# Weights of a later product split during the attention and kept in DRAM, and two column blocks of that product begun without one row block

## The chip, the core and the metric

The kernel runs on one core of one Trainium2 chip. The core has engines that each follow their own queue of instructions and meet through semaphores: TensorE (PE in the profile; its weight loads are PEld), VectorE (DVE), ScalarE (ACT), GpSimd (POOL) and SyncE (SP). Here SP computes nothing: it issues the DMAs of `load` and `store`, in its order. PE's work here is matrix products and the transposes by which tiles are turned. The metric is the device time of one execution in microseconds, as the median of several executions. All data is float32.

## What is computed

Two layers run on 640 tokens: 512 of one prompt and 128 of eight sample streams with 16 each. Layer 0 is stick-breaking attention over keys of the stream (and, for the samples, 512 cached keys each); layer 1 is gated linear attention (GLA). Each layer normalises its input, scales and shifts it by values from a conditioning vector, projects it, mixes, multiplies by a gate, projects back and adds to the residual.

```python
for i in range(DEPTH):                       # two layers
    shift, scale, gate = jnp.split(c @ w_ada[i] + b_ada[i], 3, axis=-1)
    h = rmsnorm(x, norm_g[i]) * (1 + scale[:, None]) + shift[:, None]
    if i % N_MIXERS == 0:                    # layer 0: 16 heads of 128
        y, k, v = sb_mixer(h, sb_w_in[j], sb_w_out[j], cache_sb_k[j], cache_sb_v[j])
    else:                                    # layer 1: 4 heads, keys of 256, values of 512
        y, S = gla_mixer(h, gla_w_in[j], gla_w_a2[j], gla_b_a[j], gla_norm_g[j], gla_w_out[j], S0)
    x = x + gate[:, None] * y

def sb_mixer(...):
    q, k, v, zg = jnp.split(h @ w_in, 4, axis=-1)
    ...
    y = (o * jax.nn.silu(zg.astype(jnp.float32))).astype(h.dtype) @ w_out

def gla_mixer(...):
    q, k, v, r, a_lr = jnp.split(h @ w_in, [nk, 2 * nk, 2 * nk + nv, 2 * nk + 2 * nv], axis=-1)
```

The change touches the time from the attention of layer 0 to the first product of layer 1, which is the first 512 columns of `v` in `gla_mixer`.

## The kernel before, in words

**Products.** A float32 product is made of three products of a faster type (`float32r`): each operand x is split by `halves` into hi (a cast, on ACT, L134) and lo = x - hi (a subtraction, on DVE, L135), and hi*hi + hi*lo + lo*hi is added up in PSUM. Weights come as raw tiles `wr` of 128x1024 (512 KB) by `wraw` and are split by `wsplit` into `wh` and `wl`, two buffers each; during the change of layers `ring3` gives every third piece the tiles `s0`, `s1` instead (the rows then say `s`). The 640 tokens are five row blocks `a` of 128: 0 to 3 are the prompt, 4 the samples.

**Attention.** Two lanes for the prompt (`prompt_lane`, one per head of a pair) and one for the samples (`sample_lane`) go through eight pairs of heads. The sample lane has 32 units: four per pair, two streams in each. A unit loads four blocks of cached keys and values (`kc` twice, `vc` twice), turns the keys on PE (L1100, 2 x 8 transposes), which ACT and DVE copy to `kt` (L1102), makes the scores (L1114, L1119), sends them through ACT and DVE (`stick`: a sigmoid pair on ACT, L963 and L964, a scan on DVE, L967, then L1120 to L1130), turns the weights (L1137, and L1138 for `a_new`, once in a unit), and multiplies by the values (L1152). The next unit's scores stand behind L1138 in PE's order. Beside them runs a filler, so that PE has work while a lane waits: first the products of two gates (`plain`, L650), then `share(g)`, the output projection of the attention in four parts `g` of four heads (two pairs) each. A share has 240 matmuls of 128x512 (L696), four groups of columns `c` by five row blocks by twelve; it needs the two pairs' outputs. Shares 0 to 2 are the filler as far as the lanes last, and run bare behind them. `y_t[a, c]`, the sums of the shares, lie in the slots t0 to t19 (`5 * c + a`).

**Order.** PE's order is written by hand: a `drive` runs the filler and `side.tick` puts lanes' steps between its matmuls by a planned clock `pe["now"]`; `side.until` runs lanes alone until a condition holds. DVE, ACT and POOL have a written order only from `in_order` on (the change of layers); elsewhere, and for SP everywhere, a scheduler places them.

**Change of layers.** `share(3)` ends a column block of the residual in each step (`add`): three DVE operations, a square on ACT for the norm, a DMA of x to DRAM, then `turn` (four transposes, L1327, and copies into `xp`, L1329) and, after the last column block, `norm(a)` (a `rstd_w` on DVE, turned by PE at L244). `last_gate` makes half of layer 1's gate meanwhile from 16 tiles `ar` of 512 KB (L1290). Then comes `six`: the first GLA product with eight blocks `j` of 256 rows of the weights, 30 matmuls each (six for a row block, L515). Its two first `j` are begun before everything is normalised: `most(j)` scales and splits the row blocks 1 to 4, then the product runs for blocks 1, 3, 4, 2 of j=0 and j=1; `rest(j)` adds row block 0, which is normalised last. From j=2 on, `until(j)` makes the scaled operands of the next `j` (`make`: `scale` of j+2, `part_up` of j+1) between the products, and the weights of the next `j` are loaded raw and split. Behind it come the products of a small matrix (`wa`, L1424) and the queries.

## Time and profile before

| what | value |
|---|---|
| median of three executions | 2473.24 us (2471.8 to 2477.05) |
| the profiled execution, its own time | 2472.03 us |
| its span in the profile | 2470.1 us |
| mean granted TensorE clock | 0.995 of full speed |
| PE busy | 2408.5 us, 98% of the span |
| DVE busy | 1581.7 us, 64% of the span |
| share of PE on the chain that ended last | 85% (DVE 4%, ACT 3%, DMA 2%) |

The page counts an engine as busy while it executes; ends of PE's instructions are modelled, so "busy" says where PE had work, and time is better read from starts of instructions far apart. A "pair" below is the stretch from one `a_new` transpose to the fourth after it. In rows of the trace `x24` is a count, a bracket at the end is idle time before the row with what ended it, `PEclk` is the granted clock and `DMA share` the mean busy share of the core's 16 DMA engines.

### The profile page before, as it was taken

How to read it: one execution, taken by the hardware profiler on the slowest of the kernel's cores; microseconds unless marked ns; L12 is line 12 of the kernel's file. 1: busy time of each engine (PE TensorE's matmuls, PEld its weight loads, DVE VectorE, ACT ScalarE, POOL GpSimd, SP SyncE). 2: the span in 40 equal slices, each digit the busy share in tenths (PEclk: the TensorE clock that was granted, in tenths of full speed). 3: DMA queues.
4: the chain of work that ended last, by engine and by line, in shares of the span. 5: the costliest groups of instructions: out<-in, count | busy, mean ns of one | idle time of the engine just before them, and what ended most of it. 6: DMA issues, size and time to landing. Idle time of an engine off the chain costs nothing.

```text
span 2470.1 us, 44598 instructions
## 1 busy us (share of the span) xinstructions
PE 2408.5 (98%) x17817; PEld 2141.9 (87%) x17817; DVE 1581.7 (64%) x2580; ACT 993.3 (40%) x1711; POOL 156.6 (6%) x405
## 2 busy tenths in 40 slices
PE   7999999999999999999999999999999999999998
PEld 4689999999999999888887767999999989977776
DVE  5765655555556656766776578766676566676556
ACT  4432222222223335555544245433333555565223
POOL 0010000000000000000000010000000132332000
PEclk8999999999999999999999999999999999999999
DMA  9966666766664348777774564444434678976634
GB/s 344 370 218 213 210 216 199 239 210 225 210 197 128 109 145 274 259 241 235 254 235 147 187 234 129 136 123 125 134 111 114 175 247 264 303 261 224 220 115 149
DMA packets 477841, 502.12 MB, mean 203 GB/s; under 512 B 26618, under 2 KB 386434, under 8 KB 477506
## 3 DMA queue, kind: packets, MB, share of 16 engines
q1 hardware_dynamic: 449042, 440.80, 56.2%
q0 software_dynamic: 14432, 46.67, 5.5%
q10 hardware_dynamic: 14160, 11.80, 1.4%
q8 instruction: 140, 2.29, 0.4%
q14 instruction: 67, 0.55, 0.1%
HBM read 410.05 MB, written 89.13 MB: 202 GB/s over the span
## 4 chain that ended last, share of the span: by engine, by line
PE 85%; DVE 4%; ACT 3%; DMA 2%; issue 1%; POOL 0%; SPq 0%; ACTq 0%; POOLq 0%; DVEq 0%
PE ps_mm L591 43%; PE ps_mm L696 11%; PE ps_mm L650 10%; PE ps_mm L365 3%; PE ps_tp L1100 2%; PE ps_tp L1579 2%; PE ps_tp L1152 1%; PE ps_tp L1056 1%; PE ps_z L1032 1%; PE ps_z L180 1%; PE ps_mm L2088 1%; PE ps_z L1114 1%; PE ps_z L222 1%; PE ps_tp L677 1%; PE ps_mm L515 1%
## 5 line engine op out<-in xcount | busy, mean ns | idle before, releaser
L591 PE MATMUL ps_mm<-sums,wh 128*128 128x320 f32 x2752 | 613.6, 311 | 1.5 <-ACT wh L134 1.5
L591 PEld LDWEIGHTS ps_mm<-sums,wh 128*128 128x128 f32 x2752 | 458.0, 188 | 10.4 <-issue 7.4
L591 PE MATMUL ps_mm<-h,wh 128*128 128x320 f32 x2064 | 461.4, 311 | 0.8 <-DVE u L597 0.8
L591 PE MATMUL ps_mm<-sums,wl 128*128 128x320 f32 x1376 | 425.2, 309 | 0.7 <-DVE wl L135 0.7
L135 DVE TENSOR_TENSOR wl<-wr,wh 128x1024 fp32r<-128x1024 f32 x193 | 236.2, 1225 | 211.1 <-ACT wh L134 208.1
L591 PEld LDWEIGHTS ps_mm<-h,wh 128*128 128x128 f32 x2064 | 343.2, 188 | 15.7 <-issue 11.0
L134 ACT CAST wh<-wb 128x1024 fp32r<-128x1024 f32 x170 | 178.4, 1049 | 431.8 <-PE ps_mm L591 368.2
L134 ACT CAST wh<-wr 128x1024 fp32r<-128x1024 f32 x193 | 202.5, 1050 | 324.8 <-PE ps_mm L591 186.8
L591 PE MATMUL ps_mm<-h,wl 128*128 128x320 f32 x1032 | 318.9, 309 | 0.0
L650 PE MATMUL ps_mm<-h,wh 128*128 128x320 f32 x1152 | 263.5, 316 | 3.5 <-DVE out L597 2.4
L591 PEld LDWEIGHTS ps_mm<-sums,wl 128*128 128x128 f32 x1376 | 258.3, 188 | 1.0 <-DVE wl L135 1.0
L135 DVE TENSOR_TENSOR wl<-wb,wh 128x1024 fp32r<-128x1024 f32 x170 | 207.8, 1222 | 51.0 <-ACT wh L134 50.6
L650 PEld LDWEIGHTS ps_mm<-h,wh 128*128 128x128 f32 x1152 | 192.0, 188 | 17.9 <-issue 8.9
L696 PE MATMUL ps_mm<-wh,ogh 128*128 128x512 f32 x450 | 196.8, 437 | 6.2 <-ACT y L704 3.0
L591 PEld LDWEIGHTS ps_mm<-h,wl 128*128 128x128 f32 x1032 | 193.8, 188 | 0.0
L650 PE MATMUL ps_mm<-h,wl 128*128 128x320 f32 x576 | 177.9, 309 | 0.0
L696 PE MATMUL ps_mm<-wh,ogl 128*128 128x512 f32 x450 | 177.0, 393 | 0.3 <-DVE ogl L135 0.3
L696 PE MATMUL ps_mm<-wl,ogh 128*128 128x512 f32 x450 | 177.0, 393 | 0.2 <-DVE wl L135 0.2
L696 PEld LDWEIGHTS ps_mm<-wh,ogh 128*128 128x128 f32 x450 | 84.9, 189 | 34.4 <-issue 15.1
L650 PEld LDWEIGHTS ps_mm<-h,wl 128*128 128x128 f32 x576 | 108.2, 188 | 0.0
L696 PEld LDWEIGHTS ps_mm<-wh,ogl 128*128 128x128 f32 x450 | 84.5, 188 | 20.2 <-DVE ogl L135 0.7
L515 PE MATMUL ps_mm<-wh,h 128*128 128x512 f32 x252 | 90.7, 415 | 5.6 <-ACT h L134 4.0
(370 smaller groups left out, 3719.6 us busy)
## 6 DMA issues: line engine op xcount, KB each, us to landing
ar<-in_w_ada_dram SPq DMA_DIRECT2D x128, 512.0 KB
wb<-in_sb_w_in_dram SPq DMA_DIRECT2D x82, 512.0 KB
ar<-in_w_ada_dram SPq DMA_DIRECT2D x128, 256.0 KB
kc<-in_cache_sb_k_dram SPq DMA_DIRECT2D x64, 512.0 KB
vc<-in_cache_sb_v_dram SPq DMA_DIRECT2D x64, 512.0 KB
wr<-in_gla_w_in_dram SPq DMA_DIRECT2D x51, 512.0 KB
wb<-in_gla_w_in_dram SPq DMA_DIRECT2D x45, 512.0 KB
wr<-in_sb_w_in_dram SPq DMA_DIRECT2D x44, 512.0 KB
```

The source lines that it names most:

```text
L134: nc.scalar.copy(hi, x)
L135: (e or dve).tensor_tensor(lo, x, hi.bitcast(F32), op=ALU.subtract)
L180: mm(acc[32 * q:32 * q + 32, :w], cT[:, kt + m, :], by(cT[:, kt + m, :], rs[m // each][:, m % each, q, :]), start=kt + m == 0, stop=kt + m ...
L222: mm(acc[32 * j:32 * j + 32, :256], cT[:, kt + m, :], by(cT[:, kt + m, :], r[:, 256 * j:256 * j + 256]), start=kt + m == 0, stop=kt + m == ...
L365: mm(acc[a], l[:, c], by(l[:, c], r[:, k2, :]), start=kt == k0 and first, stop=kt == k0 + nk - 1 and last)
L515: mm(acc[a], l, by(l, r[:, e, :]), start=j == 0 and e == 0 and begun, stop=j == 7 and e == 1 and last)
L591: mm(acc, l[:, k, :], by(l[:, k, :], r), start=start and k == 0 and first, stop=k == 7 and last, skip_group_check=True)
L650: mm(acc[nt], l[:, k, :], by(l[:, k, :], r), start=k0 == 8 and k == 0 and first, stop=k0 == 0 and k == 7 and last)
L677: turn_block(tp[:, c:c + P], block(out[hh][:, t0:t0 + P]), ident)
L696: mm(acc, l, by(l, r[:, e, :]), start=i == 0 and e == 0 and first, stop=i == 1 and e == 1 and last)
L1100: turn_block(tp[:, P * c:P * c + P], block(kc[:, c, P * hh:P * hh + P]), ident)
L1579: mm(out, l[a], by(l[a], r[b]), start=start and n == 0, stop=stop and n == 2, skip_group_check=True)
```

## The change

There are three edits.

1. **`presplit`**, a fourth lane during the attention. It starts when the two gates are done. For each of 16 blocks of 128 rows of the first GLA product's weights it loads a 128x512 tile (256 KB), splits it with `halves`, and stores both halves (256 KB each) to new DRAM tiles `six_d`. Its tiles are the slots t14 to t19, in two sets of three. `share(0)` gets a call `at` that, ahead of its third column group, runs lanes alone until all 16 blocks are split, since that group's and the fourth's sums use the same slots.
2. **`made(j)`** takes the place of load and split in `six`: it loads `wh` and `wl` of a block (two loads of 512 KB instead of one), and ACT and DVE no longer split them.
3. **The order at the change of layers.** `most(j)` leaves out row block 3, which `third(j)` adds; j=0 and j=1 begin with blocks 1, 4 and 2, then come (0, 3) and (1, 3) and block 0. `add` of row block 0 in the last column group is kept back (`late`) until `most(0)` is done; (0, 1) of the product, which stands for j=0 and a=1, is begun as soon as share 3's last (1, 3) is added, and so stands ahead of the last turns. The bias of the last gate is added 6 us later in the plan; x and `h21_d` stores of this stage are issued by POOL instead of ACT; `make(2)` and `make(3)` put `part_up` ahead of the next `scale`.

```diff
+    six_d = [[dp.tile([P, 1024], F32, name=f"six_{j}_{n}") for n in range(2)] for j in range(8)]
...
@@ class Quarters: most
-            scaled(t, i, j, ts, bc, P)
+            scaled(t, i, j, ts, bc, P, 3 * P)
+            samples_scaled(t, i, j, ts, bc)
+            yield
...
-            nc.scalar.dma_start(out=h21_d[i][:, j, :], in_=ts[0][:, hs[1]])
+
+        def third(self, i, j, xT, t, bc):
+
+            ts = self.exact[j]
+            scaled(t, i, j, ts, bc, 3 * P, NP)
+            halves(self.upper[j][:, 0, :NP - HALF], self.upper[j][:, 1, :NP - HALF], ts[0][:, HALF:NP])
+            halves(*[x[:, 3 * P:NP] for x in self.whole[j]], ts[1][:, 3 * P:NP])
+            move(h21_d[i][:, j, :], ts[0][:, hs[1]])
@@ six
-        parts = [(j, a) for j in range(first) for a in (1, 3, 4, 2)] + [(j, 0) for j in range(first)]
+        parts = [(j, a) for j in range(first) for a in (1, 4, 2)] + [(j, a) for a in (3, 0) for j in range(first)]
...
+                if made:
+                    if j < 7:
+                        ws[j + 1] = made(j + 1)
@@ attention
+        def presplit():
+            while not state["free"]:
+                yield step(1.0)
+            src1 = A["gla_w_in"][0].rearrange("(kt p) n -> p kt n", p=P)
+            for kt in range(KT):
+                x, *t = [slot(14 + 3 * (kt % 2) + n, (P, 512), dt, "six") for n, dt in enumerate((F32, F32R, F32R))]
+                load(x, src1[:, kt, 2 * NK:2 * NK + 512])
+                yield step(4.0)
+                halves(*t, x)
+                for d, y in zip(six_d[kt // 2], t):
+                    store(d[:, 512 * (kt % 2):512 * (kt % 2) + 512], y.bitcast(F32))
+                yield step(4.0)
+            state["split"] = True
...
-        for x in (prompt_lane(0), prompt_lane(1), sample_lane()):
+        for x in (prompt_lane(0), prompt_lane(1), sample_lane(), presplit()):
...
-            drive(share(g, og0, w_out0))
+            drive(share(g, og0, w_out0, at=lambda c: side.until(lambda: "split" in state) if c == 2 else None))
@@ last_gate
+            yield step(6.0)
             dve.tensor_tensor(bias, acc[:, :256], bias, op=ALU.add)
@@ most, add
-            while min(done[1:]) < 5:
+            while not (normed[1] and normed[2] and normed[4]):
...
+        def add(a, c, pt):
+            if (a, c) == (0, 3):
+                late.append(pt)
+                return
+            summed(a, c, pt)
+            squared(a, c)
+            if (a, c) == (1, 3):
+                next(gemm)
@@ made
+            ws = [(sp if third else wp).tile([P, 1024], F32R, tag=t, name=t[:2], bufs=1 if third else 2)
+                  for t in (ring3["tags"] if third else ("wh", "wl"))]
+            for t, d in zip(ws, six_d[j]):
+                load(t.bitcast(F32), d)
@@ behind share 3
+        side.until(lambda: busy["most"])
+        summed(0, 3, late[0])
+        squared(0, 3)
+        parts(1)
+        for _ in h2.most(1, 1, xT, xp[1], bc, middles[1]):
+            pass
+        parts(2)
+        side.until(lambda: normed[3])
+        for j in range(2):
+            h2.third(1, j, xT, xp[j], bc)
+        parts(5)
+        side.until(lambda: normed[0])
         for j in range(2):
             h2.rest(1, j, xT, xp[j], bc)
+        parts(2)
...
-            if j < 7:
+            if 3 < j < 7:
                 h2.scale(1, j + 1, xT, bc, pairs_of=lambda n: xp[n])
             if j < 8:
                 h2.part_up(1, j, pm.tile([P, 512], F32R, tag=("vhi", "vlo")[j % 2], name="middle")[:, :256])
+            if 2 <= j < 4:
+                h2.scale(1, j + 1, xT, bc, pairs_of=lambda n: xp[n])
```

In PE's order the first edit moves matmuls of the shares. Rows of one sample unit in the middle of the attention, from its scores on, before the change (L696 are the share's matmuls; L1114 and L1119 are the unit's scores, L1152 its values, L1056 and L1049 the prompt lanes):

```order
L1114 MATMUL ps_z<-kt,q_one 32x256 x8
L1119 MATMUL ps_z<-k,q 32x16 x4
L1152 MATMUL ps_tp<-vc,aT_s 32x128 x16
L1152 MATMUL ps_tp<-v,aT_s 32x128 x4
L696 MATMUL ps_mm<-wh,ogh 128x512
L696 MATMUL ps_mm<-wl,ogh 128x512
L696 MATMUL ps_mm<-wh,ogl 128x512
L1056 MATMUL ps_tp<-aT,v 128x128 x3
L1049 MATMUL ps_tp<-ident,s_12067 128x128 x3
L696 MATMUL ps_mm<-wh,ogh 128x512
L696 MATMUL ps_mm<-wl,ogh 128x512
L696 MATMUL ps_mm<-wh,ogl 128x512
```

and the same unit after the change (L1134, L1139, L1172, L1076, L1069, L1052 and L1120 are the lines that were L1114, L1119, L1152, L1056, L1049, L1032 and L1100; L1120 turns the next unit's keys, L1182 belongs to the last unit's values):

```order
L1134 MATMUL ps_z<-kt,q_one 32x256 x8
L1139 MATMUL ps_z<-k,q 32x16 x4
L1172 MATMUL ps_tp<-vc,aT_s 32x128 x16
L1172 MATMUL ps_tp<-v,aT_s 32x128 x4
L1076 MATMUL ps_tp<-aT,v 128x128 x3
L1069 MATMUL ps_tp<-ident,s_12113 128x128 x3
L1052 MATMUL ps_z<-k,q 128x512
L1120 MATMUL ps_tp<-ident,kc 128x128 x8
L1076 MATMUL ps_tp<-aT,v 128x128 x3
L1052 MATMUL ps_z<-k,q 128x512
L1120 MATMUL ps_tp<-ident,kc 128x128 x8
L1182 MATMUL ps_tp<-ident,osb 128x128
```

Of the 32 units, those that had share matmuls before had 21 or 27 each (9 and 12 in the first and the last of them). Now, after the first six of them (120 matmuls, the first two column groups of share 0), eight units have none and the one behind them has 15, so that 192 matmuls that stood in units before stand behind the last unit. In all, PE has as many matmuls as before.

SP's order in the same part of the attention, before:

```order
L71 DMA wr<-in_sb_w_out_dram 128x2x512
L71 DMA vc<-in_cache_sb_v_dram 128x4x256 x2
L71 DMA kc<-in_cache_sb_k_dram 128x4x256 x2
L71 DMA zg<-zd_135 128x1280
L71 DMA vc<-in_cache_sb_v_dram 128x4x256 x2
L71 DMA wr<-in_sb_w_out_dram 128x2x512
L71 DMA kc<-in_cache_sb_k_dram 128x4x256 x2
L71 DMA q<-qd_120 128x1280
L71 DMA k<-kd_128 128x1280
```

and after, from one load of cached values to the next but one (`six` is a tile of presplit; L71 loads, L74 stores; the two stores of a block stand behind its load and so behind its split):

```order
L71 DMA vc<-in_cache_sb_v_dram 128x4x256 x2
L71 DMA kc<-in_cache_sb_k_dram 128x4x256 x2
L71 DMA six<-in_gla_w_in_dram 128x512
L71 DMA zg<-zd_135 128x1280
L74 DMA six_0_149<-six 128x512
L74 DMA six_1_150<-six 128x512
L71 DMA vc<-in_cache_sb_v_dram 128x4x256 x2
L71 DMA six<-in_gla_w_in_dram 128x512
L71 DMA wr<-in_sb_w_out_dram 128x2x512
L71 DMA kc<-in_cache_sb_k_dram 128x4x256
L74 DMA six_0_151<-six 128x512
L74 DMA six_1_152<-six 128x512
```

The 16 loads and 32 stores of presplit lie like this between the loads of nine units: the first right behind the keys of the eighth unit, the last behind those of the seventeenth.

PE's order at the change of layers, from the last matmul of share 3, before (L244 a norm's turn, L1290 the gate, L1327 a turn of x, L515 the GLA product):

```order
L696 MATMUL ps_mm<-s_15826,ogl 128x512
L244 MATMUL ps_tp<-ident,rstd_w 128x128
L1290 MATMUL ps_z<-ar,c_15307 32x256 x8
L1327 MATMUL ps_tp<-ident,y 128x128 x4
L515 MATMUL ps_mm<-wh,h 128x512
L515 MATMUL ps_mm<-wl,h 128x512
L515 MATMUL ps_mm<-wh,h 128x512 x2
L515 MATMUL ps_mm<-wl,h 128x512
L515 MATMUL ps_mm<-wh,h 128x512 x2
```

and after, from the first matmuls of the product (L535 is that line now, L1356 and L1325 are the turn and the gate, L245 the norm):

```order
L535 MATMUL ps_mm<-wh,h 128x512
L1356 MATMUL ps_tp<-ident,y 128x128 x4
L1325 MATMUL ps_z<-ar,c_15451 32x256 x8
L535 MATMUL ps_mm<-wh,h 128x512
L535 MATMUL ps_mm<-wl,h 128x512
L535 MATMUL ps_mm<-wh,h 128x512 x2
L535 MATMUL ps_mm<-wl,h 128x512
L535 MATMUL ps_mm<-wh,h 128x512
L245 MATMUL ps_tp<-ident,rstd_w 128x128
L535 MATMUL ps_mm<-wh,middles 128x512
L535 MATMUL ps_mm<-wl,middles 128x512
L535 MATMUL ps_mm<-wh,middles 128x512
```

Before, the last two groups of the gate and a turn stood ahead of the first matmul of the product. Now its first row block, (0, 1), comes right behind share 3; a turn and the gate's last group follow, then (0, 4), the norm of block 3, and (0, 2), whose halves are the tiles `middles`.

More of the change, by code (lines that the diff above doesn't have):

```diff
@@ L482, in again, with six @@
                     halves(self.upper[n + e][:, 0], self.upper[n + e][:, 1], r[:, e])
-    def six(h, w, n0, acc, until, asked, first=0):
+    def six(h, w, n0, acc, until, asked, first=0, made=None):
         src = w.rearrange("(kt p) n -> p kt n", p=P)
@@ L1263, in hybrid_step_kernel @@
         dve.tensor_copy(cT1[:, :, :NSEQ], c91.rearrange("p r kt -> p kt r"))
-        busy = {"n": 0, "of": 0, "most": 0}
-        done = [0] * TOK
+        busy = {"of": 0, "most": 0}
+        normed = [False] * TOK
+        late = []
         def last_gate():
@@ L1294, in last_gate @@
                 store(gate_d[1][:, 1024 + 256 * j:1280 + 256 * j], bias[32 * j:32 * j + NSEQ, :])
-        def counted(gen, a):
-            busy["n"] += 1
-            yield from gen
-            busy["n"] -= 1
-            done[a] += 1
-        def most():
-            while min(done[1:]) < 5:
-                yield step(0.3)
-            for j in range(2):
-                h2.most(1, j, xT, xp[j], bc, middles[j])
-                yield step(3.0)
-                busy["most"] += 1
+        def most():
+            while not (normed[1] and normed[2] and normed[4]):
+                yield step(0.2)
+            for _ in h2.most(1, 0, xT, xp[0], bc, middles[0]):
+                yield step(0.8)
+            busy["most"] = 1
         bc = po.tile([P, T], F32, name="rstd_bc1")
@@ L1370, in hybrid_step_kernel, with made @@
         acc = []
-        gemm = six(h2, w_in1, 2 * NK, acc, until, lambda: None, 2)
+        def made(j):
+            n = ring3["n"] = ring3["n"] + 1
+            third = ring3["pool"] is not None and n % 3 == 0
+            ws = [(sp if third else wp).tile([P, 1024], F32R, tag=t, name=t[:2], bufs=1 if third else 2)
+                  for t in (ring3["tags"] if third else ("wh", "wl"))]
+            for t, d in zip(ws, six_d[j]):
+                load(t.bitcast(F32), d)
+            return [t.rearrange("p (a n) -> p a n", a=2) for t in ws]
+        gemm = six(h2, w_in1, 2 * NK, acc, until, lambda: None, 2, made)
         def ahead(c):
@@ L1379, in hybrid_step_kernel, with parts @@
         drive(share(3, og0, w_out0, add, ahead, first))
-        acc += [bank("mm") for _ in range(5)]
-        for n in range(8):
-            side.until(lambda: busy["most"] > n // 4)
-            if n == 0:
+        at = {a: bank("mm") for a in (1, 4, 2, 3, 0)}
+        acc += [at[a] for a in range(TOK)]
+        def parts(n):
+            for _ in range(n):
                 next(gemm)
-            next(gemm)
-            side.tick()
-        side.until(lambda: not busy["n"])
+                side.tick()
+        side.until(lambda: busy["most"])
[10 more added lines that the diff above has]
+        side.until(lambda: normed[0])
         for j in range(2):
             h2.rest(1, j, xT, xp[j], bc)
+        parts(2)
+        side.until(lambda: not side.lanes)
         only_d.close()
@@ L1404, in make @@
         def make(j):
-            if j < 7:
+            if 3 < j < 7:
                 h2.scale(1, j + 1, xT, bc, pairs_of=lambda n: xp[n])
```

52 lines of the change are left out of this document (32 added, 20 removed).

## The prediction

> **What bounds the kernel now.** I read first the page's head and its chain of the work that ended last, to see whether there is one engine whose work is the time.
>
> ```profile
> span 2470.1 us, 44598 instructions
> ...
> PE 2408.5 (98%) x17817; PEld 2141.9 (87%) x17817; DVE 1581.7 (64%) x2580; ACT 993.3 (40%) x1711; POOL 156.6 (6%) x405
> ...
> PE 85%; DVE 4%; ACT 3%; DMA 2%; issue 1%; POOL 0%; SPq 0%; ACTq 0%; POOLq 0%; DVEq 0%
> ```
>
> PE is the bound nearly everywhere: 85% of the chain, and busy for all but 62 us of the span. The number of PE's matmuls is the same before and after. So time can come only out of stretches where PE waits, and is lost wherever the change makes PE wait. I therefore read the two stretches that the change touches: the attention, and the change of layers. First the attention, as busy time of the engines in three stretches that run from one `a_new` transpose to another (four units with filler; one unit with only 18 short matmuls of a gate as filler; one with only nine matmuls of a share).
>
> ```profile
> core 0: us, PE busy (x) PEld busy (x) DVE busy (x) ACT busy (x) POOL busy (x), PEclk, DMA share, GB/s
> 1060.81:1110.93 50.12, 50.12 (x504) 40.93 (x503) 35.01 (x85) 29.83 (x67) 1.45 (x14) 1.00 0.75 241
> 1027.39:1036.80 9.41, 9.41 (x125) 8.69 (x123) 3.82 (x12) 5.13 (x11) 0.66 (x4) 1.00 0.79 271
> 1036.80:1048.36 11.56, 8.72 (x100) 5.93 (x99) 10.86 (x30) 6.72 (x16) 0.20 (x2) 1.00 1.00 336
> ```
>
> With its filler PE never waits: 50.12 of 50.12 us. With nine matmuls as filler (third row) it was busy for 8.72 of 11.56 us, though that unit's DVE also did splits that are not its own. What PE waited for in that unit is in its table of waits:
>
> ```profile
> PE ps_tp L1100 <- DVE kt L1102: 1.2, 1, 1.2
> PE ps_tp L1049 <- DVE s L1035: 0.9, 1, 0.9
> PE ps_mm L696 <- ACT ogh L134: 0.4, 1, 0.4
> PE ps_mm L696 <- DVE ogl L135: 0.3, 1, 0.3
> ```
>
> The first two are a unit's own chain, through DVE. The filler is what hides it.
>
> **Part 1: eight units without filler.** The order of PE takes 192 share matmuls out of the sample units and puts them behind the last one. What a unit costs PE without them:
>
> ```profile
> L696 PE MATMUL ps_mm<-wh,ogh 128*128 128x512 f32 x30 | 14.5, 483 | 0.0
> L135 DVE TENSOR_TENSOR wl<-wr,wh 128x1024 fp32r<-128x1024 f32 x3 | 3.7, 1223 | 0.7 <-ACT wh L134 0.7
> ...
> 1372.05 14.13 PE ps_mm L696 x60
> ```
>
> The first row is one of three alike (hi and lo), so four units hold 90 share matmuls, 22.5 a unit. The last row, of the chain, has 60 of them bare in 14.13 us: 0.2355 us each. A filled unit takes 50.12 / 4 = 12.53 us, so PE's own work in it is 12.53 - 22.5 x 0.2355 = 7.23 us. The 192 matmuls are worth 192 / 22.5 = 8.53 units. Behind the attention they cost 192 x 0.2355 = 45.2 us, exactly what they cost now. So the loss is 8.53 x (T - 7.23), where T is the time of a unit alone.
>
> The trace of before has no unit without any filler. Bounds for T: from below 7.23 (no wait at all: 0), and, since DVE's own work must fit too, (35.01 - 3.7) / 4 = 7.8 us (loss 4.9); from the nearest rows 9.41 us, the unit with 18 gate matmuls, and 11.56 - 9 x 0.2355 = 9.44 us, the unit with nine matmuls (loss 18.6 to 18.9). Following one unit's chain by hand (scores, mask, sigmoids on ACT, scan and products on DVE, turn, with DVE's two `kt` copies in between) I come to 8.4 to 9.2 us. I take 9.1, near the two rows, because PE then waits for work that both rows already show late: **+16 us**, with the ends 0 and +19.
>
> **Part 2: presplit's transfers.** Its ACT and DVE work (16 splits of 128x512) lies where DVE is busy for 35.01 of 50.12 us, beside PE's filler; I cost it at nothing there, and if that cover were gone each split would delay a unit by its DVE half. Its DMAs do not hide so easily. 16 x (256 KB in, 512 KB out) is 12.58 MB, on SP's queue between the keys and values of nine units, most of them units that still have filler.
>
> ```profile
> wr<-in_sb_w_out_dram SPq DMA_DIRECT2D x3, 512.0 KB
> ...
> 1440.00:1450.00 10.00, 8.77 (x64) 5.75 (x63) 6.42 (x12) 3.78 (x11) 1.10 (x2) 1.00 1.03 414
> ```
>
> In the four filled units the DMA engines moved 241 GB/s x 50.12 us = 12.08 MB, in 75% of the time: 321 GB/s while busy. Without the three `wr` of that stretch (1.57 MB) a unit's own loads are 2.63 MB, 8.2 us. At that rate presplit takes 39.2 us; at the 414 GB/s of the row above (the loads of `ar`, with longer rows) 30.4 us. Free are 0.25 x 12.53 = 3.1 us in each of five filled units, nothing in the stretch before (its share is 1.00), and 9.1 - 8.2 = 0.9 in some one and a half units alone: 17 us. So 13 to 22 us do not fit. The lead of the keys, loaded about one unit ahead (9 to 12.5 us), swallows most of it. What is left is 1 to 13 us of PE waiting for `kc`; I take **+5**, toward the lower end since presplit's rows of 512 lie between the keys' 256 and the 1024 of `ar`, and a wait here covers part of a chain wait counted above. Queued behind a store that waits for its split are the next unit's `kc` and `vc` on SP; PE's transposes (L1100) wait for those.
>
> The Trainium skill ("DMA: Bandwidth & Descriptors", section Specifications) gives about 358 GB/s as the limit of one core to HBM, by which presplit would take 35 us and 18 us would not fit, an estimate from that page. The trace disagrees with it as a ceiling: 414 GB/s in the row above. The keys' 321 to 336 lie below it. The sum goes by the rows.
>
> **Part 3: the bare shares.** 192 more matmuls run with nothing beside them, and each group ends in a DVE sum. In the bare stretches of now the waits for that sum are in the table below (`DVE y L701`, 1.6 us in three). For 45 us of bare work I take the same: **+1.5**, from 0 to 3.
>
> **Part 4: the change of layers.** PE's waits from 1335 to 1535 us (summed, times, longest), the clock there, and the rows that mark the stretch:
>
> ```profile
> PE ps_mm L515 <- ACT h L134: 5.1, 3, 3.0
> PE ps_mm L696 <- DVE y L701: 1.6, 3, 0.9
> PE ps_mm L515 <- ACT wh L134: 1.4, 1, 1.4
> PE ps_z L1290 <- DMA ar<-in_w_ada_dram: 1.2, 2, 0.7
> PE ps_mm L515 <- DVE wl L135: 1.1, 2, 0.8
> PE ps_tp L1327 <- ACT xp L1329: 0.7, 1, 0.7
> PE ps_mm L515 <- DVE s L135: 0.3, 1, 0.3
> ...
> 1460.00:1470.00 10.00, 6.82 (x50) 4.18 (x50) 7.31 (x21) 4.67 (x14) 1.10 (x2) 0.90 0.36 140
> 1470.00:1480.00 10.00, 9.63 (x43) 7.59 (x42) 7.97 (x19) 6.78 (x17) 0.00 (x0) 0.93 0.31 79
> ...
> 1461.81 0.38 PE L244 MATMUL ps_tp<-ident,rstd_w 128*128 128x128 f32 x2
> ...
> 1466.81 0.50 PE L515 MATMUL ps_mm<-wh,h 128*128 128x512 f32 x1 [3.03 <-ACT h L134]
> ...
> 1531.20 9.09 PE L1424 MATMUL ps_tp<-h,wa 128*32 128x320 f32 x61
> ```
>
> Between the end of share 3 (1461.81) and the end of the product (1531.20) the waits of L515 sum to 5.1 + 1.4 + 1.1 + 0.3 = 7.9 us. The clock lost 10% of one stretch of 10 us and 7% of the next, 1.7 us, right behind the wait of 3.03. That is 9.6 us to be had at most. Of it the change removes: the 3.03 and the slow clock behind it, since (0, 1) now stands ready when share 3 ends; the 1.4 + 1.1 + 0.3 for `wh`, `wl` and `s`, since the weights come split. ACT and DVE are eight splits of 128x1024 lighter (1.22 us of DVE each, by the row of L135 above), beside PE's work.
>
> What comes late next: (0, 4) and (1, 1) wait for DVE, which has the held-back sum of (0, 3) in front of the second `most`; j=0's block 0 still waits for the last norm. A DVE step there is at most about the 1.22 us of that split; I count 1.5 us. And SP has 1 MB for `made(0)` where 512 KB stood, ahead of the last tiles of `ar`; the gate's waits for `ar` (1.2 us in two) grow by about 1 MB / 414 GB/s = 2.5 us, of which PE, with share 3 beside it, feels I think 1.5. So 9.6 - 1.5 - 1.5 = 6.6: **-6.5 us**, with the ends -9.6 and 0 (if the late chain takes the place of the whole wait). The products behind, to which PE goes without a break, keep the gain. The moves of stores to POOL's queue, busy for 6% of the span, cost nothing, and if POOL were late only DRAM copies needed much later would be.
>
> The Trainium skill ("TensorE: Matmul & The Clock Gate", Part 1) says that after an idle window of about 3.4 us PE runs at half clock for about as long. The trace shows the fall behind one wait of 3.03 us, 1.7 us lost, so here a somewhat shorter wait was enough. The units alone have waits of at most 1.2 us in the rows above, and would stay at full clock; waits for keys might not.
>
> **Sum**, against the profiled execution's own 2472.0 us (its span is 2470.1; it lies 1.2 us below the median of 2473.24, within the runs' 2471.8 to 2477.05): 2472.0 + 16 + 5 + 1.5 - 6.5 = **2488 us**.
>
> **Rivals.**
>
> *Faster: the units need no filler.* If PE's order alone hides a unit's chain, T is about 7.3; if the transfers also fit into the lead and the change of layers loses nothing new, 2472 + 0.6 + 1.5 - 9.6 = **2464.5**. For it: PE's own work is 7.23 us a unit, and DVE's only 7.8. Against it: both light units took over 9.4 us. With the transfers free and the whole 9.6 gained it is measurably faster for T under 7.6: 8.53 x 0.37 + 1.5 - 9.6 = -5. Chance 0.17.
>
> *Near cancelling.* T at DVE's bound of 7.8 and transfers that cost 1 us: 2472 + 4.9 + 1 + 1.5 - 6.5 = **2473**. The whole band within 0.2% (2467 to 2477) is this case. Chance 0.16.
>
> *The transfers are the bound.* If DMA moves presplit at the keys' rate, and each store that waits for its split holds the keys behind it, PE waits 13 us for `kc`, twice for over 3 us with 1.7 us of half clock behind it, and T is 9.44: 2472 + 19 + 13 + 3.4 + 1.5 - 6.5 = **2502**. For it: DMA was at 1.00 and 0.75 in the units concerned. Chance 0.17.
>
> *The change of layers gains nothing*, its new order meeting the same late norm: 2472 + 16 + 5 + 1.5 = **2494.5**. It lies in the forecast's band.
>
> **How the numbers follow.** Forecast (2477 to 2498, with the last rival): 0.50; then 0.17, 0.16 and 0.17. The range leaves out the lower part of the first rival and the far side of the third, about 0.09 each: 2465 to 2502. A difference of 0.2%, 5 us, is about what a measurement of this kernel can tell from none. Faster 0.17, same 0.16, slower 0.50 + 0.17 = 0.67.
>
> **What would show it.** In the changed profile, `a_new` transposes 12.5 us apart in the units with filler and about 9.1 apart in eight; PE waits there for `DVE kt`, `s` and, at presplit's end, `DMA kc`; DMA share near 1.0 through presplit. At the change of layers no wait of 3 us, a granted clock of 1.00, no waits for `wh` or `wl` on ACT and DVE, and some 6 us less from share 3's end to L1424's first matmul. Part 1 is wrong if the eight units take under 7.8 us; part 2 if PE never waits for `kc`; part 4 if a wait for `h` of 3 us stays.

## The result, and the profile after

The changed kernel takes 2494.35 us, the median of six executions (2492.08 to 2496.84), against 2473.52 us of before (six executions, 2471.8 to 2477.05): a ratio of 1.0081, 95% interval 1.0069 to 1.0093; by the medians it is 20.8 us slower. The forecast was 2488, 2465 to 2502.

The page of the profiled execution, which took 2496.84 us, has the same matmuls and more time between them:

```profile
span 2495.1 us, 44759 instructions
...
PE 2418.6 (97%) x17817; PEld 2147.0 (86%) x17817; DVE 1583.9 (63%) x2598; ACT 995.5 (40%) x1729; POOL 160.8 (6%) x412
...
PE 81%; DVE 4%; DMA 4%; ACT 3%; issue 1%; POOL 0%; SPq 0%; ACTq 0%; POOLq 0%; DVEq 0%
```

The span grew by 25.0 us, PE's busy time by 10.1, and the share of DMA on the chain of the work that ended last went from 2% to 4%. Where the time went is read by comparing when the same instruction starts in both profiles. The table gives how late it is after the change. The 192 matmuls that the hold moved are set to their price behind the attention, 45.2 us.

| from, to | late at its end | change in it | forecast |
|---|---|---|---|
| start, to `a_new` of the last unit before the hold | +6.4 | +6.4 | +5 |
| the units without filler | +19.4 | +13.0 | +16 |
| rest of the attention, bare shares, to share 3's first turn | +19.9 | +0.5 | +1.5 |
| share 3, from its first turn to its last matmul | +26.7 | +6.7 | +1.5 |
| GLA product, from there to the wa product | +18.2 | -8.5 | -8.0 |
| layer 1 | +25.0 | +6.8 | 0 |

The first three lines come from the `a_new` rows of the two profiles and the first turns of share 3. Before:

```profile
1110.93 0.27 PE L1138 MATMUL ps_tp<-ident,a_new 128*128 128x128 f32 x1
...
1223.45 0.27 PE L1138 MATMUL ps_tp<-ident,a_new 128*128 128x128 f32 x1
...
1395.98 0.60 PE L1327 MATMUL ps_tp<-ident,y 128*128 128x128 f32 x4
...
1461.58 0.39 PE L696 MATMUL ps_mm<-s,ogl 128*128 128x512 f32 x1
```

and the same instructions after, down to the first matmul of the wa product:

```profile
1115.94 0.27 PE L1158 MATMUL ps_tp<-ident,a_new 128*128 128x128 f32 x1
...
1197.63 0.27 PE L1158 MATMUL ps_tp<-ident,a_new 128*128 128x128 f32 x1
...
1415.90 0.60 PE L1356 MATMUL ps_tp<-ident,y 128*128 128x128 f32 x4
...
1464.16 0.64 PE L1325 MATMUL ps_z<-ar,c 128*32 128x256 f32 x8 [0.82 <-DMA ar<-in_w_ada_dram]
1472.73 1.95 PE L1325 MATMUL ps_z<-ar,c 128*32 128x256 f32 x16 [4.50 <-DMA ar<-in_w_ada_dram]
1488.23 0.39 PE L716 MATMUL ps_mm<-s,ogl 128*128 128x512 f32 x1
1489.03 0.50 PE L535 MATMUL ps_mm<-wh,h 128*128 128x512 f32 x1 [0.41 <-ACT h L135]
1549.39 9.53 PE L1494 MATMUL ps_tp<-h,wa 128*32 128x320 f32 x64
```

At the first of these rows the change is 5.01 us late, and 6.4 with the six matmuls (1.4 us) that this unit had lost already. From the first to the second row it took 81.69 us instead of 112.52, without 186 matmuls worth 43.8: 13.0 us lost. The 6.4 us ahead of the hold did not go in the units with much filler. The unit with only nine share matmuls took 16.26 us between its `a_new` rows instead of 11.56, 4.7 more, and the two units ahead of it took 2.1 more; ahead of these the kernel was 0.6 us early. In the profile of after, the thin unit runs from the first to the last of these rows:

```profile
1038.24 0.27 PE L1158 MATMUL ps_tp<-ident,a_new 128*128 128x128 f32 x1
...
1044.95 1.97 PE L1120 MATMUL ps_tp<-ident,kc 128*128 128x128 f32 x8 [3.16 <-DMA kc<-in_cache_sb_k_dram]
...
1054.50 0.27 PE L1158 MATMUL ps_tp<-ident,a_new 128*128 128x128 f32 x1
```

The four units behind it, with 21 or 27 share matmuls each, took 50.05 us together instead of 50.11, though about half of presplit's traffic ran beside them.

The wait of 3.03 us ahead of the product is 0.41 now, and from share 3's end to the wa product 61.16 us pass instead of 69.62. But a wait of 4.50 us for an `ar` tile stands in share 3, and these are the granted clock and the DMA engines around it, with one stretch where presplit began:

```profile
1040.00:1050.00 10.00, 6.43 (x68) 5.14 (x62) 5.75 (x17) 4.61 (x10) 0.00 (x0) 0.83 1.01 352
...
1080.00:1100.00 20.00, 20.00 (x221) 16.48 (x214) 15.34 (x37) 12.44 (x27) 0.98 (x8) 1.00 1.05 387
...
1460.00:1470.00 10.00, 7.40 (x47) 4.96 (x45) 5.49 (x11) 2.77 (x10) 1.64 (x3) 1.00 1.02 345
1470.00:1480.00 10.00, 7.27 (x35) 5.05 (x36) 1.14 (x4) 1.61 (x5) 1.16 (x2) 0.66 0.90 341
```

The clock column (0.83 and 0.66) marks two places of half clock that were not there before: behind a wait of 3.16 us for `kc` at 1045, and behind the 4.50 us. In the filled units (1080 to 1100) the DMA share is at 1.05, where it was 0.75, and PE was busy for 20.00 of 20.00 us.

### The profile page after: what moved, and what is told of

The parts are those of the page before. It is cut to its first block, busy times and chain, and to the rows that moved or that the text cites. A ratio compares the mean times of both kernels' runs of the same rounds, so it can differ in the third digit from the quotient of the medians.

```text
span 2495.1 us, 44759 instructions
## 1 busy us (share of the span) xinstructions
PE 2418.6 (97%) x17817; PEld 2147.0 (86%) x17817; DVE 1583.9 (63%) x2598; ACT 995.5 (40%) x1729; POOL 160.8 (6%) x412
## 4 chain that ended last, share of the span: by engine, by line
PE 81%; DVE 4%; DMA 4%; ACT 3%; issue 1%; POOL 0%; SPq 0%; ACTq 0%; POOLq 0%; DVEq 0%
PE ps_mm L611 42%; PE ps_mm L716 9%; PE ps_mm L670 9%; PE ps_mm L369 3%; PE ps_tp L1120 2%; PE ps_mm L535 2%; PE ps_tp L1649 2%; PE ps_z L181 1%; PE ps_tp L1172 1%; PE ps_tp L1076 1%; PE ps_mm L2158 1%; PE ps_z L1052 1%; PE ps_z L223 1%; PE ps_z L1134 1%; DMA ar<-in_w_ada_dram 1%
## 5 line engine op out<-in xcount | busy, mean ns | idle before, releaser
L136 DVE TENSOR_TENSOR wl<-wr,wh 128x1024 fp32r<-128x1024 f32 x187 | 228.9, 1225 | 214.7 <-ACT wh L135 213.3
L135 ACT CAST wh<-wr 128x1024 fp32r<-128x1024 f32 x187 | 196.1, 1049 | 341.5 <-PE ps_mm L611 190.2
L716 PEld LDWEIGHTS ps_mm<-wl,ogh 128*128 128x128 f32 x450 | 85.3, 189 | 14.3 <-DVE wl L136 1.1
```

The costliest lines, as they stand in the source:

```text
L135: nc.scalar.copy(hi, x)
L136: (e or dve).tensor_tensor(lo, x, hi.bitcast(F32), op=ALU.subtract)
L716: mm(acc, l, by(l, r[:, e, :]), start=i == 0 and e == 0 and first, stop=i == 1 and e == 1 and last)
```

## The experiments

Each kernel ran beside before on the same chip, in 4 to 12 executions; not all ran on one chip. Ratios are to before, with 95% intervals. "Share 3's end" is the start of its last matmul, before 1461.58; "the product's stretch" goes from there to the wa product, before 69.62 us.

| kernel | ratio | share 3's end, late by | product's stretch |
|---|---|---|---|
| changed, first time | 1.0081 (1.0069 to 1.0093) | 26.7 | 61.2 |
| again | 1.0077 (1.0056 to 1.0099) | 25.7 | 61.1 |
| order_only | 1.0016 (1.0006 to 1.0026) | 2.1 | 73.2 |
| hold_only | 1.0082 (1.0065 to 1.0098) | 11.7 | 73.6 |
| presplit_only | 1.0088 (1.0071 to 1.0105) | 20.9 | 69.6 |
| load_split | 1.0111 (1.0094 to 1.0129) | 26.9 | 69.6 |
| late_split | 1.0102 (1.0087 to 1.0117) | 31.7 | 69.5 |
| free_made | 0.9991 (0.9981 to 1.0000) | 4.8 | 61.1 |
| made_pool | 1.0045 (1.0029 to 1.0062) | 21.5 | 61.1 |
| hold_c3 | 1.0091 (1.0075 to 1.0107) | 28.1 | 61.1 |
| best1 | 1.0066 (1.0045 to 1.0088) | 23.8 | 61.2 |
| tail_split | 0.9995 (0.9986 to 1.0004) | 3.2 | 61.2 |
| tail_late | 0.9989 (0.9980 to 0.9997) | 4.7 | 61.2 |

**again**: no edit.

> The changed kernel once more, unchanged. In its first profile PE was 25.1 us late at the end, but only 18.2 us late at the first matmul behind the GLA product; 6.9 us more went in layer 1, where the order of every engine is that of before. If those 6.9 us belong to that one execution (a transfer that landed late), this profile shows about 18 to 21 us at the end and the 2.66 us wait of a share's matmul for ACT is gone or elsewhere. If they belong to the change (transfers of layer 1 that fall differently against PE), the same waits stand at the same places, about 25 us. Median expected 2494 (2492 to 2497) either way.

Its profiled execution took 2490.13 us. It was 25.7 us late at share 3's end and 17.3 at the wa product, within 1 us of the first profile, but only 18.3 at the end. PE's waits in layer 1, as sum, times and longest, in this profile:

```profile
PE ps_mm L716 <- ACT y L724: 1.9, 1, 1.9
PE ps_mm L369 <- DVE y L721: 1.5, 1, 1.5
```

In the first profile the first of these lines was `5.3, 3, 2.7`. So 5.8 of the 6.8 us of layer 1 are not there in a second execution of the same program. The median is 20.8 us above before, between the two profiled executions (25.0 and 18.3), so a part of some 2.5 us in the average execution is not excluded.

**order_only**: the new order, weights raw as before, no presplit.

```diff
-        for x in (prompt_lane(0), prompt_lane(1), sample_lane(), presplit()):
+        for x in (prompt_lane(0), prompt_lane(1), sample_lane()):
...
+            for n in (j, j + 1):
+                if n < 8 and n not in raws:
+                    raws[n] = wraw(src[:, 2 * n:2 * n + 2, 2 * NK:2 * NK + 512], 2, 512)
+            return lambda: wsplit(raws[j], 2)
...
```

`made(j)` now loads the raw weights and gives back a call that splits them on ACT and DVE; `six` makes that call ahead of the products of j.

> The new order at the change of layers alone: no presplit, no hold, weights loaded raw and split on ACT and DVE as before. Theory A (the order is good, but the split weights, 1 MB for j=0 ahead of the last eight ar tiles on SP, made the gate wait 5.3 us for ar and brought the half clock): without them ar waits stay near 1.2 us, and the stretch from share 3 to L1424's successor gains 5 to 8 us: 2465 to 2468.5. Theory B (the order itself moves PE into the waits for ar, by having share 3 start its last group earlier or by the early row block): waits for ar of about 5 us here too, and 2471 to 2474.

Neither held. The waits for `ar` were short (1.5 us in three), as theory A had it, but the product's stretch grew to 73.2 us. PE started its first row block early and then waited for splits behind it:

```profile
1472.88 0.50 PE L543 MATMUL ps_mm<-wh,h 128*128 128x512 f32 x1 [2.07 <-ACT h L135]
...
1499.46 0.80 PE L543 MATMUL ps_mm<-wh,h 128*128 128x512 f32 x1 [4.36 <-ACT wh L135]
```

With the weights split on the spot the new order is worth nothing; ACT and DVE are late instead, here by 4.36 us for `wh`. So the new order alone does not bring the 8.5 us; whether the split weights would bring them in the old order was not run. My way of putting the splits into the new order is one of several, so the size of this loss is not settled, its kind is.

**hold_only**: the hold, without presplit's transfers and splits.

```diff
-                x, *t = [slot(14 + 3 * (kt % 2) + n, ...
-                load(x, src1[:, kt, 2 * NK:2 * NK + 512])
                 yield step(4.0)
-                halves(*t, x)
-                for d, y in zip(six_d[kt // 2], t): ...
                 yield step(4.0)
...
```

The weights are loaded raw and split at the change of layers, as in order_only.

> The hold of share 0 for the planned time of presplit, but presplit loads, splits and stores nothing; weights are loaded raw and split at the change of layers, in the new order. Theory A (a unit alone is limited by its own chain through DVE and ACT): the eight units without filler still take 8.5 to 8.9 us each and the attention loses 11 to 14 us; the 6.1 us ahead of them (units that wait for kc) are gone. Theory B (units alone are slow because presplit's transfers and splits are beside them): they take 7.3 to 7.8 us and the attention loses under 5 us. Time, with the order's own gain from the run beside it: A 11 to 14 us above that run, B under 5 above it.

Theory A held for the units. The same two `a_new` transposes as above (L1166 in this kernel):

```profile
1108.30 0.27 PE L1166 MATMUL ps_tp<-ident,a_new 128*128 128x128 f32 x1
...
1190.14 0.27 PE L1166 MATMUL ps_tp<-ident,a_new 128*128 128x128 f32 x1
```

81.84 us pass between them, 81.69 in the changed kernel: 13.1 and 13.0 us lost. The eight units took 8.7 us each here and 8.8 there. So the hold costs 13 us without presplit's traffic. (Some 1.3 us of them are a lower clock here, 0.93 from 1160 to 1180, which the changed kernel does not have.) Whether that traffic costs anything beside a unit alone is not shown by this pair, since little of it lies there. In the changed kernel presplit's splits on DVE say, with the first and the last start at the end:

```profile
L136 DVE TENSOR_TENSOR six<-six x16: 680/692/693, 1014.7 to 1126.6; 128x512 fp32r<-128x512 f32 x16
```

The last of the 16 starts at 1126.6 and its stores are issued at once, by 1127.3, but the hold, whose length stands in PE's order by the planned clock, goes on to 1197.63. Seven of the eight units thus went without filler for work that was all but done. A hold that ends with the splits, with all else as it is, was not run; at 8.8 - 7.23 us a unit it would save some 11 us, an estimate from these rows and the prediction's 7.23.

Before the hold this kernel was 2.6 us earlier than before, the changed one 5.0 us later. Of these 7.6 us, 1.2 lie ahead of presplit's first load, so some 6.5 us is what presplit costs in the units that still have filler, most of it in the unit with nine share matmuls (16.26 us there, 11.56 here). What binds a unit alone was not settled. In this stretch the DMA share was 0.88, and PE's longest waits were 3.0 us in three for `kc` and 1.4 for `aT`, so the unit's own loads (the 2.63 MB, 8.2 us, of the prediction) and its chain may well end near the same time. The ratio, 1.0082, is 0.66% above order_only's, 16 us and above theory A's 11 to 14. The profiled execution took 2487.8 us and the other three 2494.2 to 2496.0, so the trace is that of the fastest, 8 us above order_only's profiled one.

**presplit_only**: presplit and the hold on the kernel of before.

> Presplit and its hold on the kernel of before; the change of layers is that of before and the split copies in DRAM are not read. If the parts add up, PE is 19.9 us late when share 3 begins and stays so: 2472 + 20 = 2492 to 2494 (plus what layer 1 may add). If the presplit's cost is partly hidden by slack behind it (a change of layers that waited anyway), less than 15 us: under 2488.

The parts add up: share 3 ends 20.9 us late, of which 5.1 come ahead of the hold and 14.7 in the units without filler, and the product's stretch is that of before to 0.1 us.

**load_split**: presplit_only without its stores.

```diff
-                for d, y in zip(six_d[kt // 2], t):
-                    store(d[:, 512 * (kt % 2):512 * (kt % 2) + 512], y.bitcast(F32))
```

> The kernel of presplit_only without its 32 stores (8 MB): hold, loads (4 MB) and splits remain, the change of layers is that of before, and the output is unchanged, since nobody reads the copies there. Share 3 ended 20.9 us late in presplit_only and 11.7 us late in hold_only. Theory A (the stores cost most of the difference, by their bytes and by holding SP's queue until the split is done): share 3 ends 12 to 14 us late, ratio about 1.0055. Theory B (the loads and the splits on ACT and DVE are what costs, since they are in the units' chains): 17 to 21 us late, ratio about 1.008.

Theory B, and more than that: with 8 MB less to move, share 3 ended 26.9 us late, 6 us later than with the stores. (The intervals of the two ratios overlap; two profiles of one kernel, after and again, differ by 0.9 us at this place.) Of the loss, 13.6 us came ahead of the hold, where presplit_only lost 5.1. What ACT waited for during presplit (sum, times, longest), in this kernel:

```profile
ACT six L135 <- DMA six<-in_gla_w_in_dram: 21.9, 12, 3.0
```

In the changed kernel that line says

```profile
ACT six L135 <- DMA six<-in_gla_w_in_dram: 7.9, 2, 4.5
```

The splits stand in ACT's order among the units' own instructions, and a split whose load has not landed holds them all. Its largest single case in the changed kernel, in ACT's timeline:

```profile
1038.73 0.50 ACT L1159 COPY aT_s<-ps_tp 128x384 f32<-128x384 f32 x1
1043.76 0.62 ACT L135 CAST six<-six 128x512 fp32r<-128x512 f32 x1 [4.53 <-DMA six<-in_gla_w_in_dram]
1044.29 0.73 ACT L1015 ACTIVATE sg<-zg 128x640 f32<-128x640 f32 x1
1044.93 0.38 ACT L983 ACTIVATE k<-ps_z 128x272 f32<-128x272 f32 x1
```

ACT stood for 4.53 us at the split, with the sigmoids of a unit (L983) behind it. With the stores gone the loads and their splits bunch into fewer units (16 splits between 1012 and 1084, in the changed kernel 1014 to 1126), so more of them are met before they have landed. The Trainium skill ("TensorE: Matmul & The Clock Gate", Part 1, Architectural detail) says that PE's queue can pull weight loads ahead and that ACT and DVE take their queues strictly in order. This row agrees for ACT.

**late_split**: presplit_only, each split moved behind the next block's load and kept there.

```diff
...
+                    nc.gpsimd.tensor_copy(t[0][:, 0:1], state["latest"])
+                    halves(*t, asked[kt - 1])
...
```

> The kernel of presplit_only with each block's split put later: the next block's load is asked for first, and a small POOL copy from the prompt lane's newest output into the split's tile keeps ACT's cast behind that output, so that it stands behind some 20 more rows in ACT's order; stores follow. Bytes, splits and hold are the same. In load_split and hold_c3 ACT stood 21.9 and 23.6 us (12 times each) waiting for presplit's loads, in the changed kernel 7.9 (2 times), and the attention lost about 15, 16 and 9 us more there than with the hold alone. Theory A (ACT, and DVE behind it, stand in order at a split whose load has not landed, and the units' sigmoids behind them): ACT's waits for six fall under 2 us and share 3 ends 12 to 14 us late, near hold_only's 11.7. Theory B (the bytes delay the keys and values, whoever waits for them): ACT's waits fall too, but share 3 still ends 18 to 22 us late, with PE waiting for kc.

Theory B. ACT's waits for the loads fell to 2.4 us, and share 3 ended 31.7 us late, the latest of all (2.4 of it from ahead of presplit). PE now waited for keys:

```profile
PE ps_tp L1102 <- DMA kc<-in_cache_sb_k_dram: 8.4, 4, 3.7
```

against 6.2 us in five in the changed kernel, 2.9 of them in the units without filler. All four waits lie in these units here, which lost 21.9 us instead of 13.0: the transfers had moved there, and the DMA share was 0.97 to 1.04. So two ways to lose are shown, each in a kernel in which the other is small: splits that stand for their load (load_split) and keys that come late behind presplit's transfers (late_split). How the 6.5 us of the changed kernel divide between them was not settled: in its unit with nine share matmuls both stand, ACT for 4.53 us at a split and PE for 3.16 us for `kc`.

**free_made**: the change of layers without its price.

```diff
-            for t, d in zip(ws, six_d[j]):
+            for t, d in zip(ws, six_d[0]):
...
+        for d, y in zip(six_d[0], og0[14]):
+            for n in range(2):
+                store(d[:, 512 * n:512 * n + 512], y[:, :512].bitcast(F32))
```

> The new order and the loads of split weights, without presplit and without the hold: every block j reads the same two DRAM tiles, which are filled once with other data behind the attention (1 MB), so the GLA product's first 512 columns are left wrong and its time is kept. It gives the change of layers without its price. Theory A (in the changed kernel share 3 lost about 5.8 us to the late ar tiles and the half clock behind them, and the stretch from share 3's end to the wa product gained 8.5): 61 us in that stretch, ar waits of about 5 us, and 2.5 us faster than before. Theory B (the ar tiles were late only because presplit had shifted the program against its transfers): ar waits near 1.3 us and 8 us faster than before.

Theory A: the wait for `ar` is there without presplit, share 3 loses 5.7 us by itself, and the kernel is 2.6 us faster than before by the medians (2474.25 and 2476.86), with an interval that reaches 1.0000. So the whole change could gain no more than about this as it stands.

```profile
PE ps_z L1328 <- DMA ar<-in_w_ada_dram: 4.1, 1, 4.1
```

**made_pool**: the split weights of j=0 asked for by POOL, later.

```diff
-                load(t.bitcast(F32), d)
+                (load if j else move)(t.bitcast(F32), d)
...
-            if (a, c) == (1, 3):
+            if (a, c) in ((1, 3), (3, 3)):
                 next(gemm)
...
-            else:
-                next(gemm)
```

> The changed kernel with the two loads of made(0) issued by POOL behind share 3's block (1, 3), and made(1) one step later, instead of by SP ahead of the last eight ar tiles. Theory A (1 MB of split weights in front of ar on SP's queue and in the DMA engines makes the gate wait 5.3 us): PE's waits for ar fall to 2 us or less, the half clock in share 3 is gone, and the kernel is 5 to 6 us faster than the changed one run beside before (ratio about 1.0055 to 1.006 against 1.008). Theory B (ar waits for its own four buffers, that is for PE, or for the queries' first weights): waits of 4 us stay, no gain; POOL's norms behind the loads may cost 1 us.

Between the two. The waits for `ar` are still 4.1 us in sum, as theory B had it, but in three pieces of at most 2.2, and without the half clock. Share 3 ends 4.2 us earlier than in again, of which 1.4 came from the attention, so that it loses 3.1 us by itself instead of 5.9. The ratio fell to 1.0045. What is left of the waits was not traced further; SP still loads the queries' first weights ahead of `ar`.

**hold_c3**: the hold only ahead of the fourth column group, presplit in five slots and 3 planned us a step.

```diff
-                x, *t = [slot(14 + 3 * (kt % 2) + n, ...
+                x, *t = [slot(n, (P, 512), dt, "six") for n, dt in
+                         ((15, F32), (16 + 2 * (kt % 2), F32R), (17 + 2 * (kt % 2), F32R))]
...
-                yield step(4.0)
+                yield step(3.0)
...
-            drive(share(g, og0, w_out0, at=lambda c: ... if c == 2 else None))
+            drive(share(g, og0, w_out0, at=lambda c: ... if c == 3 else None))
```

> The changed kernel with presplit in five slots (t15 to t19, one raw tile and two pairs of halves) and three planned us per step instead of four, so that share 0 is held only ahead of its fourth column group. 81 instead of 192 matmuls leave the sample units. Theory A (each unit without filler costs what its own chain takes over PE's 7.23 us): the attention loses 81 / 22.5 = 3.6 units x 1.5 = 5.4 us for the units instead of 13, 7 to 8 us less than the changed kernel, if the transfers cost the same. Theory B (the transfers bind: the same 12.6 MB in less time): as much as is saved on units is lost waiting for kc, and it stays within 3 us of the changed kernel.

Theory B by the time, but not by its wait. 81 instead of 192 matmuls left the units, and share 3 began 22.0 us late instead of 19.9. Units with filler took up to 16.3 us beside presplit, where they take 12.2 to 13.3 without it. PE's waits in the attention, though, were short for `kc` and long for ACT, which stood 23.6 us (12 times) for presplit's loads:

```profile
PE ps_tp L1172 <- ACT aT_s L1159: 8.9, 6, 2.4
PE ps_tp L1120 <- DMA kc<-in_cache_sb_k_dram: 2.2, 3, 1.1
```

So what the shorter hold saved went to splits that stand for their load, as in load_split.

**best1**: hold_c3 and made_pool together, and stores one step behind their split.

> All of it together: hold only ahead of the fourth column group, presplit's stores one planned step behind their split, made(0) by POOL. If the parts add up: 20 us over before, less 7.5 (units), less 5.5 (ar and half clock), less up to 6 (SP no longer held by stores that wait for their split): 1 to 8 us slower than before, 2474 to 2481 by the runs of before of the first time. If DMA binds all of presplit: 10 us slower.

1.0066: the parts do not add up, since the hold's saving had already gone in hold_c3. Against that kernel share 3 ends 4.3 us earlier, much as made_pool's does against again (4.2); the intervals of the two ratios overlap.

**tail_split**: no hold. Presplit runs when the last keys are turned, beside the bare part of share 2, in tiles of the rings of `kc` and `vc`; the rest is made_pool.

```diff
-            while not state["free"]:
+            while "turned" not in state:
...
+                x = kp.tile([P, 2, 512], F32, tag="kc", name="six")
+                t = [at.tile([P, 2, 512], F32R, tag="vc", name="six", bufs=4) for _ in range(2)]
...
```

> No hold: presplit runs behind the last unit's keys, beside the bare part of share 2, in tiles of the kc and vc rings, 512 KB loads and stores; share 0 to 2 lie as before; made(0) by POOL, the new order at the change of layers. In the profile of before the DMA engines were busy for 0.00 to 0.62 from 1320 to 1390, DVE under 0.65, so 12.6 MB (30 to 39 us) and eight splits should fit. Theory A (place, not amount, made presplit dear): attention as before, up to 2 us of new waits in share 2, the stretch from share 3's end to the wa product 61 us instead of 69.6, ar waits up to 4 us: 3 to 7 us faster than before (ratio 0.997 to 0.999). Theory B (the transfers also bind here: share 2's and 3's weights wait behind the stores on SP): share 3 starts 5 to 10 us late and nothing or less is left (ratio 1.000 to 1.003).

Theory A for the trace (share 3 ends 3.2 us late, the product's stretch 61.2), less for the time: 0.9995, which is no difference that eleven executions can tell.

**tail_late**: the same, each split behind the last unit's output.

> tail_split with every split kept behind the last sample unit's output by the same kind of POOL copy, and 2.5 planned us a step. In tail_split PE stood 1.9 us for the last unit's osb and ran at 0.91 to 0.92 of the clock from 1330 to 1350, and share 3 ended 3.2 us late; behind it 8.4 us were gained. Theory A (splits ahead of the last units' work on ACT and DVE): that wait and the half clock are gone, share 3 ends 0 to 2 us late, ratio 0.997 to 0.999. Theory B (the transfers themselves are late for the shares): share 3 ends 3 us late or more, ratio 0.999 to 1.001.

The wait for `osb` and the half clock behind it went. Share 3 ended 4.7 us late, as theory B had it, but not for its reason: it began only 1.0 us late by its first turn, and lost 3.7 us by itself, where PE's waits for `ar` (2.7 us) and `xp` (2.5) were 3.3 us longer than before. The stretch in which presplit ran:

```profile
1330.00:1340.00 10.00, 9.38 (x81) 6.97 (x79) 6.66 (x12) 5.02 (x9) 0.38 (x2) 1.00 0.04 17
1340.00:1350.00 10.00, 9.15 (x50) 7.46 (x49) 8.19 (x10) 4.23 (x7) 1.27 (x2) 1.00 1.00 349
1350.00:1360.00 10.00, 9.63 (x42) 7.66 (x42) 5.51 (x7) 4.20 (x4) 0.37 (x2) 1.00 1.01 379
1360.00:1370.00 10.00, 10.00 (x44) 8.10 (x44) 5.74 (x7) 2.10 (x2) 0.33 (x2) 1.00 1.00 384
```

Of the kernels that compute the whole result it has the lowest ratio, 0.9989 (0.9980 to 0.9997), some 3 us below before and 0.9% below the change; its interval overlaps tail_split's. Its splits and stores all lie between 1337 and 1377, where PE has dense work that waits for nobody but its own sums.

## Why the prediction was right

Its sign and its main term held. Some sizes did not, two of them in opposite ways, so that the nearness of the sum is in part luck.

- **Part 1**, units without filler, +16 forecast, 13.0 measured, and 13.1 with the hold alone. The units alone take 6.5 to 11.2 us in the changed kernel and 8.8 on average (8.7 in hold_only), not 9.1; the two rows from which 9.1 came, the unit with gate matmuls and that with nine share matmuls, bounded it from above. The rival that needs T under 7.6 is refuted.
- **Part 2**, transfers, +5 forecast, 6.4 against before and some 6.5 against hold_only measured. The size was near, the place was not. The forecast saw too little room for the transfers beside the filled units, and waits for `kc` at presplit's end; but the filled units lost nothing, and PE waited 3.3 us for `kc` at presplit's start, in the unit with the least filler. And one sentence of the working was wrong: presplit's splits were costed at nothing because DVE has room beside them. Their busy time is indeed hidden, but ACT stands in order at a split until its load has landed, 7.9 us here, 21.9 in load_split. The transfers also went faster than the 321 GB/s that I had put first, up to 387 in the filled units.
- **Part 3**, bare shares, +1.5 forecast, 0.5 measured with the rest of the attention.
- **Part 4**, -6.5 forecast, -1.7 measured. The step that failed is "of which PE, with share 3 beside it, feels I think 1.5": share 3 lost 6.7 us, 4.1 of it longer waits for `ar` and the rest half clock behind a wait of 4.50 us. That the loads of the split weights of j=0 are the cause, the experiments show together. Share 3 by itself loses 5.7 to 6.7 us in the four kernels in which SP asks for them ahead of `ar` (the change, again, free_made, hold_c3), 0.9 to 3.7 in the four in which POOL asks for them later, and 0.6 or less where the same order has raw weights (order_only, hold_only). The other half was sized well: 9.6 less 1.5 were to be had, and 8.5 came, the same to 0.1 us in eight kernels with the new order and split weights. "ACT and DVE are eight splits lighter, beside PE's work" understated it: order_only shows that without that the new order loses.
- **The sum** was 16 + 5 + 1.5 - 6.5 = 16 against 18.2 at the wa product in the profile of after. The errors of parts 1 and 4, -3 and +4.8, partly cancel. The rest of the way from 2488 to 2494.35 is 1.5 us by which the profiled execution of before lay under its median, and 2.6 us by which the difference of the medians exceeds 18.2, which was not traced.
- **The rivals.** That in which the transfers bind did not come: PE waited 6.2 us for `kc`, not 13. late_split, with 8.4, is nearest to it; hold_c3, with 2.2, is slow for another reason. The rival in which the change of layers gains nothing named 2494.5, which the median meets to 0.2 us, but by luck: the late norm on which it rested did not come (0.41 us is left of the 3.03). The gain came, and the wait for `ar` took most of it back.

## What to carry to other kernels

Work that is moved to "where there is room" brings its waits along: an engine that takes its queue in order stands at a split until the load has landed, and everything behind it stands too, however low the engine's busy time is. Filler on PE can cover such waits: in the changed kernel the well-filled units lost nothing beside full DMA engines and the thin one 4.7 us, but in hold_c3, where more splits stood for their loads, filled units lost too. Look for a stretch in which the transfers' own path is idle (here the DMA share of 0.00 to 0.62 behind the last unit), not only for one in which the engines are. If a filler is what hides a chain, price every hold of the filler as its time alone less its own work: 8.5 units times 1.5 us here. And look in the trace when the work is done for which the hold is there; here it was done 70 us before the hold ended.

## What the runs showed of the hardware

- The Trainium skill ("TensorE: Matmul & The Clock Gate", Part 1) gives an idle window of about 3.4 us, after which PE runs at half clock. Shorter waits of PE were followed by half clock here: 3.03 us before (1.7 us lost), 3.16 us for `kc` after (0.83 of the clock over 10 us), 2.39 us in hold_only (0.93 over 20 us), 2.07 in order_only (0.83 over 10 us) and 1.89 in tail_split (0.91 to 0.92 over 20 us). Others of about that length were not: 2.20 us in made_pool's share 3 and 1.92 us in layer 1 of before, both at 1.00. A wait of 4.50 us for `ar` was followed by 0.66 over 10 us. Where it was paid, the price came to half of the wait or more, and from some 1.9 us on it is open whether it is paid.
- Two executions of the same program differed by 6.7 us in span, and by 5.8 of it behind the wa product, with the order of every engine the same. Waits of share matmuls for ACT in layer 1 (5.3 us in three against 1.9 in one) are 3.4 us of the difference. A single profile cannot carry a claim of 5 us in that stretch.
- Taking 8 MB of stores out of a stretch with full DMA engines did not make it faster: load_split was 26.9 us late at share 3's end, presplit_only 20.9. Its splits had bunched, and ACT stood 21.9 us for their loads instead of 7.6.
